# The first layer norm's sum centred before the last two parts of an output product, and the means of its weights made in small pieces

## The chip, the cores and the metric

The program runs on one core of a Trainium2 chip, in one launch. The metric is the device time of that launch in microseconds (us). The engines are named as the profile names them: PE (matrix products; PEld loads its weights), DVE, ACT and POOL (elementwise work), SP (here it only issues DMAs).

## What is computed

One step of a two-layer decoder for 576 token columns (512 of a prompt, 8 samples of 8), width 1024. Layer 0 mixes with two head groups, A (RWKV-7) and B (retention); their outputs are concatenated and go through one output product. The change sits at the end of that mixer: the output product, and the layer norm on what it adds to the residual.

```python
def layer_norm(x, g, b):
    xf = x.astype(jnp.float32)
    mu = jnp.mean(xf, -1, keepdims=True)
    var = jnp.mean(jnp.square(xf - mu), -1, keepdims=True)
    return ((xf - mu) * lax.rsqrt(var + LN_EPS)).astype(x.dtype) * g + b

y = jnp.concatenate([ya, yb], axis=-1).astype(x.dtype) @ w_out   # layer 0; ya, yb: 512 wide each
x = layer_norm(ALPHA * x + y, ln1_g[l], ln1_b[l])
x = layer_norm(ALPHA * x + sqrelu_mlp(x, w_up[l], w_down[l]), ln2_g[l], ln2_b[l])
```

## The kernel before

Activations lie with the width on the 128 partitions (8 tiles `x[0..7]`) and tokens along the free axis, in two groups of 288 columns (`g` = 0, 1). To keep float32 accuracy a factor is split into a high and a low part, and a product is three matrix products (`mm3`, lines 152 to 154: high by high, high by low, low by high). Plain float32 products (the norm's sums, the centring) go through PE in two passes.

**The mixer stage.** Twelve generators each issue one strand of work: the input projection (30 column blocks, `acc` on lines 152 to 154), the head pairs of A (`pres`, `stages`, four `back`s with the block inverse L803, the scan L863, the outputs L872/L875 and `ya`), the samples, the retention fronts and backs of B, and `wout`, the output product. `drive` steps through them. Before, the table `SCHEDULE` lists for each step which generator goes on and at which priority; the framework then orders each engine's queue by these priorities and by what is ready. An engine's queue runs strictly in order.

**The output product.** Its eight blocks k of 128 input rows come in four parts: (0, 1, 2), (3, 4, 5), (6), and 7. `Wout.part` splits the inputs of its blocks, then for each of 8 output tiles m fetches weight pieces (`wr`, two buffers; a piece is 128 x 256 or 128 x 128), splits them on ACT (L1306) and POOL (L1307), accumulates in PSUM tile `wa` and adds it to `x[m]` on DVE (L1336 in the first part, L1338 after). Part (0, 1, 2) waits for `ya2`, part (3, 4, 5) for `ya3` and the first two retention pairs, part (6) for the third. `Wout.keep`, run after the first part, fetches and splits the eight weight pieces of block 7, which stay in SBUF as `kh`, `kl`.

**The first layer norm.** `trunk` makes the products of block 7 (`acc<-hh,kh`) and hands each to `ln_add`: DVE adds it to x (L244 for m = 0, L257 for the others); for m = 0 a product over the 128 rows of `x[0]` (`cps`, L246) gives a rough mean that is taken off all eight tiles (L255: seven per group on POOL, one on DVE); then PE sums each tile (`ps`) and ACT's square of it (`pq`), both on L283. `ln_finish` makes mean and 1/deviation, then per tile subtracts and multiplies (L309 DVE, L310 POOL or DVE), scales and shifts on ACT (L313), and splits into high (L77 ACT) and low (L78 DVE).

**After it.** The first four blocks of the MLP's up product (`acc<-he,wh` and the like, 192 products of 288 columns) take x of group 0 and then of group 1; `sums` makes differences of x tiles on POOL (L1564, 16 of them), split to `ht`, `lt`; all following blocks come in pairs of seven half products (`gemm7`) that need these. The first `gemm7` product with them is `acc<-ht,wh`. `evac_up` takes relu (ACT L1588), squares (DVE L1589) and splits an up block.

Of the kernel before, what the change touches and what calls it, by code (L numbers as in the profile page):

```python
# [24 lines left out]
class Trunk:  # L25
# [252 lines left out]
    def ln_mm(self, st, n, g, t, stop):  # L278
        k = (g, n, 'ps')
        start = k not in st  # L280
        if start:
            st[k] = self.p_misc.tile([P, GN], F32, tag="misc", name='p' + n)
        self.nc.tensor.matmul(st[k], lhsT=self.ones1024, rhs=t, start=start, stop=stop)  # L283

# [938 lines left out]
def post(o):  # L1223
# [12 lines left out]
SCHEDULE = (  # L1236
# [36 lines left out]
def drive(tc, *gens):  # L1273

    base = tc.cur_priority
    for c, p in SCHEDULE:
        tc.cur_priority = base + p
        next(gens[c], None)
    tc.cur_priority = base + max(p for _, p in SCHEDULE) + 10000

# [65 lines left out]
def build(tc, i, o, coff):  # L1346
    nc = tc.nc
    T = Trunk(tc, i['w'], ahead=2)
    with ExitStack() as es:
# [9 lines left out]
        with ExitStack() as s1:  # L1359
# [121 lines left out]
            def wout():  # L1481
                for n, (ks, ns) in enumerate(WP):
# [4 lines left out]
                    if n == 0: W.keep()  # L1487
# [223 lines left out]
```

## Time and profile before

| what | us |
|---|---|
| three timed runs, median (lowest to highest) | 1575.98 (1573.06 to 1576.76) |
| the profiled execution, whole | 1570.47 |
| its span in the trace | 1568.7 |
| PE busy in the span | 1476.0 (94%) |
| DVE busy | 1077.6 (69%) |
| ACT busy | 639.8 (41%) |
| POOL busy | 564.0 (36%) |

Busy time is the union of an engine's instruction spans. Products on PE overlap each other, so the distance between the starts of two of them, and not the span of one, tells how fast they go. A number in square brackets at the end of a timeline row is the idle time of the engine before it and what ended it.

### The profile page before, as it was taken

How to read it: one execution, taken by the hardware profiler on the slowest of the kernel's cores; microseconds unless marked ns; L12 is line 12 of the kernel's file. 1: busy time of each engine (PE TensorE's matmuls, PEld its weight loads, DVE VectorE, ACT ScalarE, POOL GpSimd, SP SyncE). 2: the span in 40 equal slices, each digit the busy share in tenths (PEclk: the TensorE clock that was granted, in tenths of full speed). 3: DMA queues.
4: the chain of work that ended last, by engine and by line, in shares of the span. 5: the costliest groups of instructions: out<-in, count | busy, mean ns of one | idle time of the engine just before them, and what ended most of it. 6: DMA issues, size and time to landing. Idle time of an engine off the chain costs nothing.

```text
span 1568.7 us, 29898 instructions
## 1 busy us (share of the span) xinstructions
PE 1476.0 (94%) x11760; PEld 1421.9 (91%) x11760; DVE 1077.6 (69%) x2038; ACT 639.8 (41%) x1345; POOL 564.0 (36%) x643
## 2 busy tenths in 40 slices
PE   6999999998997889999999998989998999999995
PEld 6999898987886689999999997889988999999995
DVE  4656766675756795664846779899799575574755
ACT  4444334332233553342624545434365244251533
POOL 2032213336443551211302377555564121121355
PEclk9999999999898889999999999999999999999998
DMA  5333234435223013231322411223402314132221
GB/s 171 96 96 91 86 101 130 139 92 168 82 64 120 0 43 121 81 122 57 106 81 68 135 42 56 74 74 115 129 1 81 97 66 135 54 121 68 83 66 61
DMA packets 71197, 140.04 MB, mean 89 GB/s; under 512 B 21744, under 2 KB 31200, under 8 KB 71056
## 3 DMA queue, kind: packets, MB, share of 16 engines
q1 hardware_dynamic: 68224, 129.69, 26.6%
q0 software_dynamic: 1536, 5.57, 1.1%
q10 hardware_dynamic: 1296, 2.86, 0.6%
q8 instruction: 92, 1.51, 0.4%
q14 instruction: 49, 0.40, 0.1%
HBM read 124.39 MB, written 13.70 MB: 88 GB/s over the span
## 4 chain that ended last, share of the span: by engine, by line
PE 77%; DVE 11%; DMA 4%; POOL 4%; issue 3%; ACT 1%; SPq 1%; DVEq 0%; ACTq 0%; POOLq 0%
PE acc L152 21%; PE acc L153 21%; PE acc L154 21%; DVE wl L78 2%; PE mx L803 2%; DMA raw<-in_w 1%; DVE u L309 1%; POOL x L255 1%; DVE hl L78 1%; PE mx L700 1%; PE wa L152 1%; PE mx L542 1%; PE pq L283 1%; PE ps L283 1%; PE wa L154 1%
## 5 line engine op out<-in xcount | busy, mean ns | idle before, releaser
L77 ACT CAST wh<-raw 128x512 fp32r<-128x512 f32 x440 | 252.7, 618 | 411.2 <-PE acc L153 269.7
L78 DVE TENSOR_TENSOR wl<-raw,wh 128x512 fp32r<-128x512 f32 x440 | 330.2, 782 | 42.2 <-ACT wh L77 34.9
L153 PE MATMUL acc<-hl,wh 128*128 128x288 f32 x1180 | 349.0, 297 | 7.1 <-DVE hl L78 7.1
L154 PE MATMUL acc<-hh,wl 128*128 128x288 f32 x1180 | 348.6, 297 | 0.0
L152 PE MATMUL acc<-hh,wh 128*128 128x288 f32 x1180 | 344.4, 297 | 2.3 <-DVE ta L205 1.8
L153 PEld LDWEIGHTS acc<-hl,wh 128*128 128x128 f32 x1180 | 222.9, 189 | 8.0 <-DVE hl L78 7.5
L152 PEld LDWEIGHTS acc<-hh,wh 128*128 128x128 f32 x1180 | 221.2, 189 | 3.2 <-DVE ta L205 2.0
L154 PEld LDWEIGHTS acc<-hh,wl 128*128 128x128 f32 x1180 | 223.0, 189 | 0.3
L152 PE MATMUL acc<-xh,wh 128*128 128x288 f32 x480 | 148.3, 310 | 13.4 <-ACT xh L1395 12.4
L123 POOL TENSOR_TENSOR s<-raw 128x512 f32<-128x512 f32 x37 | 56.0, 1515 | 272.4 <-DMA raw<-in_w 206.1
L153 PE MATMUL acc<-xl,wh 128*128 128x288 f32 x480 | 146.2, 305 | 0.0
L154 PE MATMUL acc<-xh,wl 128*128 128x288 f32 x480 | 146.0, 304 | 0.0
L152 PE MATMUL acc<-ht,wh 128*128 128x288 f32 x444 | 130.9, 296 | 1.7 <-ACT wh L77 1.3
L153 PE MATMUL acc<-lt,wh 128*128 128x288 f32 x444 | 130.7, 295 | 0.0
L154 PE MATMUL acc<-ht,wl 128*128 128x288 f32 x444 | 130.5, 295 | 0.0
L123 POOL TENSOR_TENSOR raw<-raw 128x512 f32<-128x512 f32 x37 | 54.6, 1475 | 157.0 <-DVE raw L123 106.6
L152 PEld LDWEIGHTS acc<-xh,wh 128*128 128x128 f32 x480 | 91.5, 191 | 16.7 <-ACT xh L1395 12.8
L153 PE MATMUL acc<-lo,wh 128*128 128x288 f32 x352 | 105.2, 299 | 0.0
L152 PE MATMUL acc<-ho,wh 128*128 128x288 f32 x352 | 104.9, 300 | 0.1
L154 PE MATMUL acc<-ho,wl 128*128 128x288 f32 x352 | 104.9, 299 | 0.0
L153 PEld LDWEIGHTS acc<-xl,wh 128*128 128x128 f32 x480 | 91.5, 191 | 2.6 <-DVE xl L1396 0.7
L154 PEld LDWEIGHTS acc<-xh,wl 128*128 128x128 f32 x480 | 91.6, 191 | 1.5 <-issue 0.2
(461 smaller groups left out, 3498.0 us busy)
## 6 DMA issues: line engine op xcount, KB each, us to landing
raw<-in_w SPq DMA_DIRECT2D x160, 512.0 KB, 3.9
raw<-in_w SPq DMA_DIRECT2D x60, 256.0 KB, 2.9
A<-stg SPq DMA_DIRECT2D x9, 288.0 KB, 2.4
x<-in_x POOLq DMA_DIRECT2D x8, 288.0 KB, 7.4
out_y<-x SPq DMA_DIRECT2D x16, 144.0 KB, 1.8
wr<-in_w SPq DMA_DIRECT2D x16, 128.0 KB, 2.3
wr<-in_w SPq DMA_DIRECT2D x32, 64.0 KB, 2.0
kr<-A SPq DMA_DIRECT2D x6, 288.0 KB, 2.7
```

The costliest lines, as they stand in the source:

```text
L77: a = self.nc.scalar.copy(hi[:, s], src[:, s])
L78: b = self.nc.vector.tensor_tensor(out=lo[:, s], in0=src[:, s], in1=hi[:, s].bitcast(F32), op=ALU.subtract)
L123: tt = lambda e, o, x, y, op: e.tensor_tensor(out=o, in0=x, in1=y, op=op)
L152: nc.tensor.matmul(acc, lhsT=hi, rhs=xh, start=first, stop=False)
L153: nc.tensor.matmul(acc, lhsT=hi, rhs=xl, start=False, stop=False)
L154: nc.tensor.matmul(acc, lhsT=lo, rhs=xh, start=False, stop=last)
L255: e.tensor_tensor(out=t, in0=t, in1=c, op=ALU.subtract)
L283: self.nc.tensor.matmul(st[k], lhsT=self.ones1024, rhs=t, start=start, stop=stop)
L309: nc.vector.tensor_tensor(out=u, in0=r, in1=mn, op=ALU.subtract)
L542: self.nc.tensor.matmul(ps, lhsT=lhsT, rhs=rhs[:, o:o + n], start=True, stop=True)
L700: nc.tensor.matmul(both[h][:, i], lhsT=b3[q, c, h:h + 2].rearrange('p s t -> p (s t)'), rhs=la[q, c], start=True, stop=True)
L803: nc.tensor.matmul(ps[:, i], lhsT=bd(self.mb if n < 3 else self.Y0, j + i), rhs=v[:, j + i], start=True, stop=True)
```

## The change

1. **Order.** `SCHEDULE` is gone; `drive` now keeps a clock for each generator, adds `RATE[c]` times what a step yields, and always steps the generator with the lowest clock that isn't waiting. For the generators other than `wout` the yields are unchanged, the resulting order is not that of the table.
2. **Means of weights.** `keep` becomes `means`, which yields between its pieces: eight pieces of two 128 x 128 blocks for the row sums of blocks 6 and 7 over all 1024 outputs (DVE reduce), then four more for block 7, from which ACT takes the mean (bias) before they are split and kept. Part (6) fetches four such double pieces and takes the mean off on ACT, where it fetched eight single ones.
3. **Centring.** After part (3, 4, 5), `center` sums each group's eight x tiles on PE against a matrix of 1/1024 and DVE takes that mean off all 16. As the weights of what is added later have no mean, x stays centred.
4. **First norm.** `ln0_add` adds, squares on ACT, adds squares in pairs on POOL for m < 6, and sums on PE five tiles per group; no `cps`, no `ps`. `ln0_finish` scales x in one DVE operation a tile, and takes high (ACT), low (DVE) and the shifted x (ACT) from it.
5. `evac_up` squares on ACT.

```diff
-SCHEDULE = (
-    (0, 100000), (1, 100000), (1, 100000), (2, 100000), (3, 100000), (4, 100000), (5, 100000), (6, 100000), (7, 100000), (8, 100000), (9, 100000), (10, 100000), (11, 100000),
...
+RATE = (735.4, 69, 94, 102.8, 96.9, 129.4, 147, 133, 167.5, 137.3, 134, 148.1)
...
+    while live:
+        ok = [c for c in live if free(c)]
+        c = min(ok, key=lambda c: (max(time[c], now) if wait[c] is not None else time[c], c))
...
+        else: time[c] += RATE[c] * (1 if y is None else y)
...
+    def ln0_add(self, st, m, g, r, a):
+        nc = self.nc
+        st[g, m] = r
+        nc.vector.tensor_tensor(out=r, in0=r, in1=a, op=ALU.add)
+        t = self.p_tmp.tile([P, GN], F32, tag="t", name="lt", bufs=self.tb)
+        nc.scalar.activation(t, r, AF.Square)
+        if m >= 6: self.ln_mm(st, 'q', g, t, m == 7)
+        elif m % 2:
+            nc.gpsimd.tensor_tensor(out=t, in0=st[g, 'q'], in1=t, op=ALU.add)
+            self.ln_mm(st, 'q', g, t, False)
+        else: st[g, 'q'] = t
+
+    def ln0_finish(self, st, g, par, out):
...
+        with self.tc.issue_after(self.pre.ins):
+            nc.scalar.activation(w0, v, AF.Ln, bias=self.eps)
+        nc.scalar.activation(w, w0, AF.Exp, scale=-0.5)
+        V.scalar_tensor_tensor(out=w0, in0=w, scalar=-0.5, in1=w, op0=ALU.mult, op1=ALU.mult)
+        V.scalar_tensor_tensor(out=v, in0=v, scalar=LN_EPS, in1=w0, op0=ALU.add, op1=ALU.mult)
+        V.scalar_tensor_tensor(out=v, in0=v, scalar=1.5, in1=w, op0=ALU.add, op1=ALU.mult)
+        gam, bet = par
+        for m in range(KT):
+            r, (hi, lo), b = st[g, m], out(m, g), bet[:, m:m + 1]
+            V.scalar_tensor_tensor(out=r, in0=r, scalar=gam[:, m:m + 1], in1=v, op0=ALU.mult, op1=ALU.mult)
+            x = nc.scalar.activation(hi, r, AF.Identity, bias=b)
+            y = V.scalar_tensor_tensor(out=lo, in0=r, scalar=b, in1=hi.bitcast(F32), op0=ALU.add, op1=ALU.subtract)
+            nc.scalar.activation(r, r, AF.Identity, bias=b)
+            if g and m == self.gated - 2: self.gate = [x.ins, y.ins]
...
-    def keep(self):
-        self.w7 = [self.weights(m, 7, 1, True) for m in range(8)]
+    def means(self):
...
+        for k in (6, 7):
+            s = self.wq.tile([P, 4], F32, name=f's{k}', bufs=1)
+            for m in range(0, 8, 2):
+                t = load(k, m)
+                yield 3
+                nc.vector.tensor_reduce(out=s[:, m // 2:m // 2 + 1], in_=t, axis=AX.XY, op=ALU.add)
+            b = self.wq.tile([P, 1], F32, name=f'b{k}', bufs=1)
+            nc.vector.tensor_reduce(out=b, in_=s, axis=AX.X, op=ALU.add)
+            nc.vector.tensor_scalar(out=b, in0=b, scalar1=-1.0 / 1024, scalar2=None, op0=ALU.mult)
+            self.less[k] = b
+        for m in range(0, 8, 2):
+            t = load(7, m)
+            yield 3
+            hi, lo = (self.wq.tile([P, 2, P], F32R, name=f'k{c}{m}', bufs=1) for c in 'hl')
+            nc.scalar.activation(t, t, AF.Identity, bias=b)
+            nc.scalar.copy(hi, t)
+            nc.gpsimd.tensor_tensor(out=lo, in0=t, in1=hi.bitcast(F32), op=ALU.subtract)
+            self.w7 += [(hi[:, x], lo[:, x]) for x in range(2)]
+
+    def center(self, mx):
...
+        for g in range(2):
+            ps = mx.tile([P, 512], F32, tag='mx', name='mx')[:, 0:GN]
+            xs = [t[:, GN * g:GN * (g + 1)] for t in T.x]
+            for m, t in enumerate(xs):
+                nc.tensor.matmul(ps, lhsT=o, rhs=t, start=m == 0, stop=m == KT - 1)
+                if m % 2: yield 1
+            for t in xs: nc.vector.tensor_tensor(out=t, in0=t, in1=ps, op=ALU.subtract)
+            yield 3
...
-                    if n == 0: W.keep()
+                    if n == 0: yield from W.means()
+                    if n == 1: yield from W.center(mxb)
...
-        nc.vector.tensor_tensor(out=t, in0=t, in1=t, op=ALU.mult)
+        nc.scalar.activation(t, t, AF.Square)
```

What moves on the engines shows best at three places. First PE, where part (3, 4, 5) of the output product begins. Before (`L542` is the gate product of pair 3's `ya`, `hd` with L969 the normed output of a retention pair; `L1074` transposes the next retention pair):

```order
L154 MATMUL wa<-hi_4610,l 128x288
L542 MATMUL mx<-gd,lw 128x288
L1131 MATMUL rpo<-rS,e 128x128
L542 MATMUL mx<-gd,lw 128x288
L969 MATMUL mx<-cst_170,hd 128x128 x4
L971 MATMUL mx<-cst_170,hd 128x64
L1160 MATMUL mx<-rvt,rkm 64x64 x16
L944 MATMUL mx<-cst_170,rot 64x128
L152 MATMUL wa<-hi_5490,h 128x288 x2
L1074 MATMUL mx<-cst_170,w_5345 128x128 x4
L153 MATMUL wa<-lo_5491,h 128x288 x2
```

Now, at the same place (L904 and L907 are the pair's outputs `po`, before L872 and L875; L1001 and L1003 a retention pair's; L524 transposes pair 3's normed output, L574 is its gate product):

```order
L154 MATMUL wa<-hi_5010,l 128x288
L904 MATMUL po<-uv_127,lr_126 64x64 x16
L907 MATMUL po<-la_125 64x64 x14
L1001 MATMUL mx<-cst_170,hd 128x128 x4
L1003 MATMUL mx<-cst_170,hd 128x64
L524 MATMUL mx<-cst_170,hd 64x64 x18
L574 MATMUL mx<-gd,lw 128x288 x2
L152 MATMUL wa<-hi_5693,h 128x288 x2
L153 MATMUL wa<-lo_5694,h 128x288
L154 MATMUL wa<-hi_5693,l 128x288
L152 MATMUL wa<-hi_5697,h 128x288
```

All other rows of the mixer now stand ahead of part (3, 4, 5); before, the last retention pair's stood between its products. Between pair 3's `po` and the part's first product PE now has 25 products.

Second PE, at the end of part (6). Before:

```order
L152 MATMUL wa<-hi_5921,h 128x288
L153 MATMUL wa<-lo_5922,h 128x288
L154 MATMUL wa<-hi_5921,l 128x288
L246 MATMUL cps<-x_4548,o_6126 128x288
L283 MATMUL ps<-x_4548,o_6125 128x288
L283 MATMUL pq<-lt,o_6125 128x288
L283 MATMUL ps<-x_4549,o_6125 128x288
L152 MATMUL acc<-hh_6160,kh_5486 128x288
```

Now:

```order
L152 MATMUL wa<-hi_6013,h 128x288
L153 MATMUL wa<-lo_6014,h 128x288
L154 MATMUL wa<-hi_6013,l 128x288
L283 MATMUL pq<-lt,o_6153 128x288 x10
L152 MATMUL acc<-he_6160,wh 128x288 x4
L153 MATMUL acc<-le_6161,wh 128x288
L154 MATMUL acc<-he_6160,wl 128x288
L152 MATMUL acc<-ho_6168,wh 128x288
```

The products of block 7 now stand among those of part (6), ahead of this place, and ten sums of squares are all that stands between the last `wa` and the up product.

Third DVE, from the last addition to x of each version on. Before:

```order
L1338 TENSOR_TENSOR x_4555<-x_4555,wa 128x288 x2
L255 TENSOR_TENSOR x_4548<-x_4548,ln 128x288
L257 TENSOR_TENSOR x_4549<-x_4549,acc 128x288
L257 TENSOR_TENSOR x_4550<-x_4550,acc 128x288
L257 TENSOR_TENSOR x_4551<-x_4551,acc 128x288
L257 TENSOR_TENSOR x_4552<-x_4552,acc 128x288
```

Now:

```order
L289 TENSOR_TENSOR x_4262<-x_4262,acc 128x288
L305 SCALAR_TENSOR_TENSOR w_6303<-w 128x288
L306 SCALAR_TENSOR_TENSOR pq<-pq,w_6303 128x288
L307 SCALAR_TENSOR_TENSOR pq<-pq,w 128x288
L311 SCALAR_TENSOR_TENSOR x_4255<-x_4255,par,pq 128x288
L311 SCALAR_TENSOR_TENSOR x_4256<-x_4256,par,pq 128x288
L311 SCALAR_TENSOR_TENSOR x_4257<-x_4257,par,pq 128x288
```

The additions of block 7 (L289) are done by then for both groups, and group 0's eight scalings (L311) and eight low parts (L313) follow without a subtraction; then come the three operations L305 to L307 and the same sixteen of group 1.

More of the change, by code (lines that the diff above doesn't have):

```diff
@@ L283, in ln_mm @@
         self.nc.tensor.matmul(st[k], lhsT=self.ones1024, rhs=t, start=start, stop=stop)
+    def ln0_add(self, st, m, g, r, a):
[10 more added lines that the diff above has]
+    def ln0_finish(self, st, g, par, out):
+        nc, V = self.nc, self.nc.vector
+        pt, v = self.p_tmp, st[g, 'q', 'ps']
+        w0, w = [pt.tile([P, GN], F32, tag="t", name=n, bufs=self.tb) for n in ('w0', 'w')]
+        with self.tc.issue_after(self.pre.ins):
[12 more added lines that the diff above has]
+            if g and m == self.gated - 2: self.gate = [x.ins, y.ins]
     def ln_finish(self, st, g, par, out, last=False):
@@ L1233, in post, with free @@
             c(sh[1:][None]), c(wk(o['swkv'])), c(rt(o['sret'])), c(cv[1:][None]))
-SCHEDULE = (
[33 rows of a table removed]
-)
-def drive(tc, *gens):
[L1275 to L1279, printed above, removed]
+RATE = (735.4, 69, 94, 102.8, 96.9, 129.4, 147, 133, 167.5, 137.3, 134, 148.1)
+def drive(tc, *gens):
+    base, n = tc.cur_priority, len(gens)
+    time, wait, live, held, now = [100000.0] * n, [None] * n, set(range(n)), set(), 100000.0
+    def free(c):
+        w = wait[c]
+        return w is None or (w() if callable(w) else w not in held)
+    while live:
+        ok = [c for c in live if free(c)]
+        c = min(ok, key=lambda c: (max(time[c], now) if wait[c] is not None else time[c], c))
+        if wait[c] is not None:
+            time[c] = max(time[c], now)
+            if not callable(wait[c]): held.add(wait[c])
+            wait[c] = None
+        now = max(now, time[c])
+        tc.cur_priority = base + int(time[c])
+        try:
+            y = next(gens[c])
+        except StopIteration:
+            live.discard(c)
+            continue
+        if callable(y): wait[c] = y
+        elif isinstance(y, tuple):
+            if y[0] > 0: wait[c] = y[1]
+            else: held.discard(y[1])
+        else: time[c] += RATE[c] * (1 if y is None else y)
+    tc.cur_priority = base + int(max(time)) + 10000
 CFG = {(n, g): dict(ds=() if n else tuple(range(8)), dq=() if n else tuple(range(8)), sv=(7,), qv=(7,), pg=(1, 2, 3, 4, 5, 6, 7), mulv=(0, 3, 6), affv=()) for n in range(4) for g in range(2)}
@@ L1298, in __init__, with weights @@
         self.T, self.nc, self.w = T, T.nc, w
-        self.w7 = []
+        self.w7, self.less = [], {}
         self.y = [None] * 8
-    def weights(self, m, k0, n, keep=False):
-        t = self.wq.tile([P, 2 * P], F32, tag='wr', name='wr', bufs=2)[:, 0:n * P]
-        self.nc.sync.dma_start(t, self.w[30 + m, :, P * k0:P * (k0 + n)])
-        hi, lo = (self.wq.tile([P, n * P], F32R, name=f'k{c}{m}', bufs=1) if keep else self.wq.tile([P, 2 * P], F32R, tag=f'w{c}', name=c, bufs=2)[:, 0:n * P] for c in 'hl')
+    def weights(self, m, k0, n):
+        t = self.wq.tile([P, 2, P], F32, tag='wr', name='wr', bufs=2)
+        b = self.less.get(k0)
+        if b is None:
+            t = t[:, 0:n]
+            self.nc.sync.dma_start(t.rearrange('p m c -> p (m c)'), self.w[30 + m, :, P * k0:P * (k0 + n)])
+        else:
+            n = 2
+            self.nc.sync.dma_start(t, self.w[30 + m:32 + m, :, P * k0:P * (k0 + 1)].rearrange('m p c -> p m c'))
+            self.nc.scalar.activation(t, t, AF.Identity, bias=b)
+        hi, lo = (self.wq.tile([P, 2, P], F32R, tag=f'w{c}', name=c, bufs=2)[:, 0:n] for c in 'hl')
         self.nc.scalar.copy(hi, t)
@@ L1308, in weights, with load @@
         return hi, lo
-    def keep(self):
-        self.w7 = [self.weights(m, 7, 1, True) for m in range(8)]
+    def means(self):
+        nc = self.nc
+        def load(k, m):
+            t = self.wq.tile([P, 2, P], F32, tag='wr', name='wr', bufs=2)
+            nc.sync.dma_start(t, self.w[30 + m:32 + m, :, P * k:P * (k + 1)].rearrange('m p c -> p m c'))
+            return t
+        for k in (6, 7):
[17 more added lines that the diff above has]
+    def center(self, mx):
+        nc, T = self.nc, self.T
+        o = self.wq.tile([P, P], F32, name='wo', bufs=1)
+        nc.gpsimd.memset(o, 1 / 1024)
+        for g in range(2):
[6 more added lines that the diff above has]
+            yield 3
     def part(self, ks, first):
@@ L1328, in part @@
                 n = min(2, len(ks) - j)
-                hi, lo = self.weights(m, ks[j], n)
+                if ks[j] not in self.less: hi, lo = self.weights(m, ks[j], n)
+                elif m % 2 == 0: two = self.weights(m, ks[j], n)
+                if ks[j] in self.less: hi, lo = (w[:, m % 2:m % 2 + 1] for w in two)
                 for g, a in enumerate(accs):
                     for x in range(n):
-                        T.mm3(a, hi[:, P * x:P * (x + 1)], lo[:, P * x:P * (x + 1)], *[c[:, GN * g:GN * (g + 1)] for c in h[ks[j + x]]], j + x == 0, j + x == len(ks) - 1)
+                        T.mm3(a, hi[:, x], lo[:, x], *[c[:, GN * g:GN * (g + 1)] for c in h[ks[j + x]]], j + x == 0, j + x == len(ks) - 1)
             for g, a in enumerate(accs):
@@ L1510, in build @@
             T.ones1024 = hp.tile([P, P], F32, name='o1'); T.ones128 = hp.tile([P, P], F32, name='o2')
+            T.eps = hp.tile([P, 1], F32, name='ep'); nc.gpsimd.memset(T.eps, LN_EPS)
             nc.gpsimd.memset(T.ones1024, 1 / 1024); nc.gpsimd.memset(T.ones128, 1 / 128)
@@ L1611, in mlp @@
             T.gemm(u + 16 * q + 8, 8, hx, res_evac(T.ln_state(ln, x), lnpar(ln), out, first=q == 0, final=q == 3), tail=TL if q == 3 else 0, far=(FAR1 if ln == 1 else 0) if q == 3 else 0)
-    ev = res_evac(T.ln_state(0, x), lnpar(0), split_x, first=False)
+    st = T.ln_state(0, x)
     T.ensure(E0)
@@ L1618, in trunk @@
             T.mm3(a, hi, lo, *hx(7, g), True, True)
-            ev(m, g, a)
+            T.ln0_add(st, m, g, x[m][:, gs[g]], a)
+        T.ln0_finish(st, g, lnpar(0), split_x)
     T.ensure(41)
```

32 rows, old and new, of the table SCHEDULE are left out of this document.

## The prediction

> **What bounds the kernel now.** First the page: PE is busy nearly throughout, so time can only come out of the places where it isn't, or out of its own work.
>
> ```profile
> span 1568.7 us, 29898 instructions
> PE 1476.0 (94%) x11760; PEld 1421.9 (91%) x11760; DVE 1077.6 (69%) x2038; ACT 639.8 (41%) x1345; POOL 564.0 (36%) x643
> ```
>
> Then the table of busy time by stretch, from the end of the input projection to where PE is full again. Columns: stretch, its length, busy us of PE, PEld, DVE, ACT, POOL (instructions), granted clock of PE.
>
> ```profile
> 314.00:353.50 39.50, 36.78 (x398) 33.06 (x398) 27.65 (x73) 12.79 (x34) 14.49 (x23) 0.91 0.34 93
> 353.50:366.10 12.60, 8.43 (x97) 7.91 (x96) 3.23 (x8) 3.69 (x9) 8.13 (x12) 1.00 0.93 325
> 366.10:443.00 76.90, 69.25 (x761) 61.95 (x761) 52.11 (x133) 25.40 (x72) 39.22 (x54) 0.88 0.28 81
> 443.00:470.00 27.00, 26.42 (x219) 24.49 (x219) 14.61 (x42) 7.73 (x25) 10.75 (x18) 0.89 0.24 70
> 470.00:497.00 27.00, 20.41 (x144) 16.87 (x143) 21.59 (x52) 10.91 (x26) 8.11 (x15) 0.93 0.46 139
> 497.00:523.00 26.00, 19.77 (x74) 13.86 (x75) 15.37 (x31) 8.20 (x19) 15.77 (x18) 0.83 0.10 36
> 523.00:543.00 20.00, 20.00 (x118) 18.31 (x116) 11.73 (x24) 10.44 (x26) 5.01 (x6) 0.89 0.00 1
> 543.00:562.80 19.80, 12.28 (x79) 11.67 (x77) 19.80 (x20) 13.03 (x31) 19.80 (x20) 0.88 0.00 1
> ```
>
> Two parts show. Up to 497 PE works off the mixer's end and the output product, with small holes. From 497 to 563 it is busy for 52 of 66 us, and in the last stretch DVE and POOL are busy without a pause: there the norm, not PE, sets the pace. The timelines of DVE and PE bound that stage:
>
> ```profile
> 496.49 0.93 DVE L1338 TENSOR_TENSOR x<-x,wa 128x288 f32<-128x288 f32 x2
> 511.36 0.46 DVE L294 SCALAR_TENSOR_TENSOR ln<-pq,d 128x288 f32<-128x288 f32 x1 [4.36 <-ACT d L292]
> 523.12 1.57 PE L152 MATMUL acc<-he,wh 128*128 128x288 f32 x4
> 562.79 0.61 PE L153 MATMUL acc<-hl,wh 128*128 128x288 f32 x1 [4.72 <-DVE hl L78]
> 571.48 0.41 PE L152 MATMUL acc<-ht,wh 128*128 128x288 f32 x1
> ```
>
> The last addition of part (6) ends at 497.42. Group 0's sums take until 511.4, the first up product starts at 523.1, and the 192 products of the four unpaired blocks are done only when the first `ht` product starts, at 571.48. So the stage takes **74.1 us**. What PE must do in it shows in the distance of starts:
>
> ```profile
> 541.13 0.29 PE L153 MATMUL acc<-lo,wh 128*128 128x288 f32 x1
> 541.26 0.29 PE L154 MATMUL acc<-ho,wl 128*128 128x288 f32 x1
> 507.02 0.65 PE L283 MATMUL ps<-x,o 128*128 128x288 f32 x2
> 507.51 0.65 PE L283 MATMUL pq<-lt,o 128*128 128x288 f32 x2
> ```
>
> A product of 288 columns takes 0.133 us, a plain float32 one (two passes) 0.49.
>
> **The norm's stage, worked anew.** It removes both `cps` and their chain, 16 `ps`, six of 16 `pq`, the subtractions L255 and L309 and the products L310; on PE 24 products of 0.49 us, 11.8 us. What is left, from the last addition on, is priced by these rows:
>
> ```profile
> 499.76 0.44 ACT L260 ACTIVATE lt<-x 128x288 f32<-128x288 f32 x1 [0.53 <-DVE x L255]
> 537.51 0.45 ACT L299 ACTIVATE w<-w 128x288 f32<-128x288 f32 x1
> 511.73 1.92 DVE L309 TENSOR_TENSOR u<-x,ln 128x288 f32<-128x288 f32 x5
> 517.08 1.04 DVE L309 TENSOR_TENSOR u<-x,ln 128x288 f32<-128x288 f32 x1
> 518.05 0.44 DVE L257 TENSOR_TENSOR x<-x,acc 128x288 f32<-128x288 f32 x1
> ```
>
> Square 0.44, sum on PE 0.65 (the row of `pq`), logarithm and exponential 0.45 each, three DVE operations of 0.46 (the row of L294), eight scalings (five take 1.92, so 3.0), the first low part 0.46: 6.9 us, with hand-overs between engines some 7.5. Then 192 products of 0.133, 25.5 us: **33 us** if nothing holds PE. What does is the way to `ht`. POOL's 16 differences need x of both groups, shifted by ACT:
>
> ```profile
> L1564 POOL TENSOR_TENSOR ts<-x,ts 128x288 f32<-128x288 f32 x8 | 8.9, 1132 | 0.0
> L1564 POOL TENSOR_TENSOR ts<-x 128x288 f32<-128x288 f32 x4 | 4.3, 1075 | 0.0
> L1564 POOL TENSOR_TENSOR ts<-x,x 128x288 f32<-128x288 f32 x4 | 4.0, 1010 | 0.0
> L123 POOL TENSOR_TENSOR raw<-raw 128x512 f32<-128x512 f32 x1 | 1.5, 1476 | 0.0
> L78 DVE TENSOR_TENSOR lt<-ts,ht 128x576 fp32r<-128x576 f32 x8 | 5.6, 746 | 0.0
> ```
>
> ACT's queue holds 37 operations or so between the first exponential (at 2.9 us) and the first shifted tile of group 1 (eight squares, sixteen high parts, eight shifts, the other group's two, some relus): at 0.4 us, 18 us. Then POOL 17.2 and one L123, 1.5, then the last `lt` 0.7: 37.4; I take **38 us**, a saving of **36**. The low end of the stage is PE's 33. For the high end: while POOL runs, a DVE operation on two SBUF tiles takes 1.04 where 0.37 is its pace alone (L309 above), one that reads PSUM stays at 0.44 (L257 between). DVE's queue has about 66 operations from the last addition to the last `lt`; half of them slowed gives 33 x 0.37 + 33 x 1.04 = 47, so 50 with the start. The saving lies between 24 and 41.
>
> The squares of `evac_up` leave DVE for ACT, which is busy 13 of 19.8 us where DVE has no pause; that is in the 38. At the second MLP I cost the same eight at nothing: only PE's queue of ready products covers them there, and without it they are worth eight times the 0.45 row, under 4 us.
>
> **The mixer's end.** Three terms move the last addition.
>
> Centring: 16 plain products of 0.49 on PE, **+7.8 us**, as PE is the busy engine there (26.4 of 27 us in 443 to 470). The 16 subtractions on DVE (0.44 each) run beside part (6)'s first products and those of block 7; uncovered, the eight of group 1 would cost 3.5.
>
> A hole before part (3, 4, 5): now nothing but 25 small products stands on PE between pair 3's `po` and the part's first product. How long the way takes shows on the timelines of PE and DVE before, where it was filled:
>
> ```profile
> 419.06 1.03 PE L875 MATMUL po<-la 64*64 64x64 f32 x28
> 420.14 0.69 DVE L989 TENSOR_REDUCE hs<-po 128x8 f32<-128x512 f32 x1 [0.38 <-PE po L875]
> 440.98 1.15 PE L1160 MATMUL mx<-rvt,rkm 64*64 64x64 f32 x32 [2.69 <-ACT hd L972]
> 443.08 0.85 PE L152 MATMUL wa<-hi,h 128*128 128x288 f32 x2 [0.62 <-ACT h L1306]
> ```
>
> From 420.1 to 443.1, 23 us of reductions, `rsqrt`, transposes, gate and splits. Now DVE has less else to do there and the 25 products fill some 2: I take **+15 us**; ends 0 (other work slips in) and 23. What stood in this place before has moved ahead and is done there, so only the idle time counts.
>
> Holes that close: before part (0, 1, 2) PE sat for its first input, and in the row above for `hd`:
>
> ```profile
> 366.10 0.54 PE L152 MATMUL wa<-hi,h 128*128 128x288 f32 x2 [4.17 <-ACT hi L1322]
> ```
>
> Both waits now have mixer rows ahead of them: 4.2 + 2.7, **-6.9 us**, or nothing.
>
> The pieces of the means: `keep` and the last pieces of the first part ran as one string of DMA issues, part (3, 4, 5) as another.
>
> ```profile
> 423.94 17.18 SPq L1304 DMA_DIRECT2D wr<-in_w x12
> 445.81 12.09 SPq L1304 DMA_DIRECT2D wr<-in_w x8
> ```
>
> 1.43 and 1.51 us each. Twelve pieces of `means` instead of eight add 4 x 1.5 = 6 us to that string, part (6) gives four back; a double piece with runs of 512 B isn't in the trace, between the 1.4 above and twice that. I cost it at nothing, since `means` stands beside pair 3's scan and the wait just priced; uncovered it is 6 to 20 us. Behind these issues in SP's queue stand the pieces of part (3, 4, 5) and the trunk's `raw` loads. The eight reductions, at most 0.69 us of DVE each by the 128 x 512 row of their kind (L989), hide there too.
>
> PE's clock after a hole bears on this: in 497 to 523 the granted clock is 0.83, and the four products from 523.12 take 1.57 us, not 0.69 as at full pace (three distances of 0.133 and the last one's 0.29). The Trainium skill ("TensorE: Matmul & The Clock Gate", "Part 1: The HAM clock gate (the "warmup" mystery)") says the clock halves after some 3.4 us idle and needs about 3.4 us of work to come back; that speaks against a change that leaves PE idle in two places. By it each costs 1.7 us, as an estimate, and the sum would be 3.4 us less of a gain; the trace agrees with the slow start.
>
> **The sum.** 7.8 + 15 - 6.9 = +15.9 at the mixer's end, -36 in the norm's stage: **-20.1 us**. The profiled execution took 1570.47 (span 1568.7 and 1.8 around it), so 1550.4; the three runs' median, 1575.98, is 5.5 above it, and against that **1556**. With the ends of its terms this case reaches from 1541 to 1573.
>
> **Rivals.**
>
> *The hole is covered*: other strands, or the means' work, fill PE while `ya` of pair 3 is made. For it: before, that stretch was 90% busy. Against: the queue is in order and holds nothing else. 7.8 - 6.9 - 36 = -35: 1541. Chance 0.22.
>
> *The gain is eaten*: DVE beside POOL sets the stage (24 saved), the hole is whole. 7.8 + 23 - 6.9 - 24 = 0: 1576, no change. The 1.04 us rows speak for it, DVE's shorter list against. Chance 0.12.
>
> *Slower, by the new order*: the table goes, and pair 2's scan now stands behind the last projection product instead of ahead of it. Before:
>
> ```profile
> 311.82 0.33 PE L863 MATMUL ch<-la 64*64 64x64 f32 x4
> 330.17 0.48 PE L863 MATMUL ch<-la 64*64 64x64 f32 x4
> L153 PE MATMUL acc<-xl,wh x480: 289/294/608, 7.6 to 353.4; 128*128 128x288 f32 x160
> ```
>
> The scan took 19 us under the projection's products, which ran until 353.4. Without them PE may sit through those 19 us; with the whole hole (23) and no hole closed: 7.8 + 23 + 19 - 36 = +14, **1590**. It decides once the mixer's end slips by more than the 36 saved. For it: retention and samples are all that is left to fill. Against: pair 3's inverse now runs beside that scan. Chance 0.14. That the sums are not saved at all is ruled out by PE's order.
>
> Forecast 0.52. A measurement of this kernel can tell about 0.3%, 4.7 us. Faster by more: 0.52 + 0.22 = 0.74; within: 0.12; slower: 0.14. The range takes in the better case with some us below it and stops halfway up the slower one: 1534 to 1583.
>
> **What the profile will show.** Right if from the last addition to x (L289) to the first `ht` product it is 33 to 45 us; if PE idles 10 us or more ahead of part (3, 4, 5); if that last addition lies 10 to 22 us later than 497. Wrong if PE's idle time between 300 and 450 grows by more than the hole (the order costs more than the norm gives), if weight pieces end the waits of part (3, 4, 5) (the means aren't covered), or if `lt` ends PE's longest wait with the stage near 50 us.

## The result, and the profile after

The changed kernel takes **1596.13 us** (median of 4 runs, 1591.37 to 1608.08), the kernel before 1574.95 us beside it (4 runs, 1573.06 to 1576.76): a ratio of 1.0144, with a 95% interval of 1.0097 to 1.0192. It is slower by 21 us (15 to 30 by the interval; its runs took 1591.4, 1591.8, 1600.5 and 1608.1 us), where 20 less were forecast. The profiled execution took 1591.37 us; the head of its page:

```profile
span 1589.6 us, 29855 instructions
PE 1486.1 (93%) x11744; PEld 1430.3 (90%) x11744; DVE 1064.8 (67%) x2040; ACT 645.8 (41%) x1355; POOL 547.8 (34%) x619
```

PE has 16 records of products fewer than before (eight plain float32 products, each in two passes), and is busy 10 us longer; the span grew by 20.9. To find where, the same two points as in the prediction, on the timelines of DVE and PE after (start, us, engine, line, operation):

```profile
547.63 0.45 DVE L1406 TENSOR_TENSOR x<-x,wa 128x288 f32<-128x288 f32 x1
548.11 0.45 DVE L289 TENSOR_TENSOR x<-x,acc 128x288 f32<-128x288 f32 x1
586.53 0.29 PE L152 MATMUL acc<-ht,wh 128*128 128x288 f32 x1
```

The last addition to x ends at 548.6 instead of 497.4: **51 us later**, where 16 were forecast. From there to the first `ht` product it takes **38.0 us** instead of 74.1, the number that was forecast. That makes 15.0 of the 20.9; the other 5.9 come behind the first `ht` product. Groups of PE's products with their waits, two before and one after, each over the 54 us from the first `ht` product on (busy us, mean ns of one | idle us ahead of them, and its end):

```profile
L152 PE MATMUL acc<-ht,wh 128*128 128x288 f32 x24 | 7.3, 304 | 1.4 <-ACT wh L77 1.3
L153 PE MATMUL acc<-lt,wh 128*128 128x288 f32 x24 | 7.1, 295 | 0.0
```
```profile
L153 PE MATMUL acc<-lt,wh 128*128 128x288 f32 x24 | 7.5, 312 | 4.0 <-DVE lt L78 4.0
```

So PE reaches the `ht` products earlier than POOL and DVE can feed the rest of them. In the first 13.5 us it waits 2.6 us longer than before, its clock is 0.87 instead of 1.00, and it makes 61 products instead of 90: some 4 us of the saving go there. Where the other 2 go was not followed.

What sets the 38.0 us is PE itself. Its first up product starts 9.0 us after the last addition (557.5), and from there to the first `ht` product it makes 216 products without a pause, 29.0 us. POOL's last difference ends at 591.2 and the last `lt` at 597.1, 48.6 us after the last addition.

Where the 51 us lie is told by the stretch from 250 us to the projection's last product, and from that to the first product of part (3, 4, 5). Before, then after (columns as in the prediction's table; behind the clock stand the DMA share and GB/s):

```profile
250.00:353.50 103.50, 100.78 (x1133) 93.19 (x1132) 78.75 (x185) 34.27 (x83) 39.20 (x48) 0.97 0.41 118
353.50:443.00 89.50, 77.68 (x858) 69.86 (x856) 55.34 (x141) 29.09 (x80) 47.35 (x66) 0.90 0.37 115
```
```profile
250.00:349.50 99.50, 93.79 (x816) 85.34 (x815) 62.74 (x144) 35.09 (x80) 35.67 (x45) 0.97 0.38 111
349.50:489.90 140.40, 111.80 (x1234) 97.25 (x1232) 85.00 (x240) 39.75 (x107) 52.67 (x72) 0.78 0.32 96
```

The second stretch grew by **50.9 us**, which equals the slip (the first is 4.0 us shorter, and from part (3, 4, 5)'s first product to the last addition it takes 58.7 us instead of 54.4, with the centring in it). It holds 376 products more than before. By their lines 208 of them belong to one head pair (its scan, outputs, norm, gate and samples), and 20 to a retention pair; these had run between the products of the projection (that stretch has 317 fewer; the others ran earlier, before 250 us) and now run after them, when there is nothing else to put between them. 147 are the last retention pair's, which before stood behind the start of part (3, 4, 5). Of the 50.9 us, 16.8 are PE's idle time (28.6 instead of 11.8) and 34.1 are busy time, at a granted clock of 0.78 instead of 0.90. The scan of pair 2 shows it on PE's timeline: before, its first and last row stood at 311.8 and 330.2, under the projection; after:

```profile
373.67 0.48 PE L895 MATMUL ch<-la 64*64 64x64 f32 x4
393.98 0.31 PE L895 MATMUL ch<-la 64*64 64x64 f32 x3
```

Behind it come pair 3's scan (its last `ch` at 456.3) and its output, and then the hole that was forecast:

```profile
469.78 1.76 PE L907 MATMUL po<-la 64*64 64x64 f32 x28
476.49 1.09 PE L1001 MATMUL mx<-cst,hd 128*128 128x128 f32 x4 [4.95 <-DVE hd L997]
481.61 2.19 PE L524 MATMUL mx<-cst,hd 64*64 64x64 f32 x36 [3.73 <-DVE hd L1038]
486.36 2.29 PE L574 MATMUL mx<-gd,lw 128*128 128x288 f32 x4 [2.57 <-ACT hd L1047]
489.91 0.85 PE L152 MATMUL wa<-hi,h 128*128 128x288 f32 x2 [1.25 <-ACT hi L1388]
```

From `po`'s end (471.5) to the part's first product it is 18.4 us, with 12.5 us of waits in brackets: a chain of DVE and ACT operations with small products between, and no other work on PE to fill the waits.

### The profile page after: what moved, and what is told of

Same layout as the page of the kernel before. It is cut to its first block, busy times and chain, and to the rows that moved or that the text cites. A ratio compares the mean times of both kernels' runs of the same rounds, so it can differ in the third digit from the quotient of the medians.

```text
span 1589.6 us, 29855 instructions
## 1 busy us (share of the span) xinstructions
PE 1486.1 (93%) x11744; PEld 1430.3 (90%) x11744; DVE 1064.8 (67%) x2040; ACT 645.8 (41%) x1355; POOL 547.8 (34%) x619
## 4 chain that ended last, share of the span: by engine, by line
PE 71%; DVE 12%; DMA 6%; POOL 4%; issue 3%; ACT 3%; SPq 1%; ACTq 0%; DVEq 0%; POOLq 0%
PE acc L152 19%; PE acc L153 19%; PE acc L154 19%; DVE wl L78 3%; DMA wr<-in_w 2%; PE mx L835 2%; DMA raw<-in_w 2%; DVE u L341 1%; PE mx L732 1%; PE wa L152 1%; POOL s L123 1%; PE wa L153 1%; PE wa L154 1%; ACT wh L77 1%; SPq L814 1%
```

## Experiments

Two theories stood against each other. **A**: the order costs it, as the table is replaced by rates and the pairs' chains are issued later. **B**: the new work costs it, the centring, the pieces of means and the hole that they make. All times below are medians beside runs of the kernel before on the same chip (1572.5 to 1573.8 us in the sets).

**The order alone.** The kernel before, with nothing but this (`drive` as in the change):

```diff
-SCHEDULE = (
...
-)
+RATE = (735.4, 69, 94, 102.8, 96.9, 129.4, 147, 133, 167.5, 137.3, 134, 148.1)
 def drive(tc, *gens):
...
```

> The kernel before with the planner's rates in place of the written table, nothing else changed: the same products, the same norm. Theory A (the order costs it): the mixer's end slipped by 51 us with the whole change, of which the centring's 16 products explain 8 and the hole ahead of part (3, 4, 5) some 15; the other 28 are the order's, and the hole is the order's too, so the last addition of part (6) comes 28 to 43 us later than 497 and the time is 1603 to 1618 us. Theory B (the new work costs it: centring, pieces of means and the hole they make; the order is nothing): 1570 to 1580 us, the last addition within 5 us of 497.

1606.5 us, ratio 1.0214 (1.0193 to 1.0235): **+33.5 us**. Its last addition ends at 533.2, its norm's stage is 73.8 us long, as before. The same stretches, of this run:

```profile
250.00:351.30 101.30, 97.21 (x828) 88.47 (x827) 62.98 (x145) 35.03 (x80) 37.01 (x45) 0.95 0.39 110
351.30:485.20 133.90, 110.56 (x1232) 96.42 (x1231) 83.30 (x228) 38.52 (x107) 53.70 (x75) 0.79 0.30 93
```

The 1232 products behind the projection are there without a centring or a mean. From part (3, 4, 5)'s first product to the last addition this run takes 48.0 us instead of 54.4, as the last retention pair is out of that stretch; the 33.5 us are the balance. Theory A stands; B falls for the larger part.

**The whole change with the old table**, 22 steps of `wout` (strand 11) added to its 424: twelve (11, 125228) for the means, ten from 129375 on for the centring.

```diff
-RATE = (735.4, 69, 94, 102.8, 96.9, 129.4, 147, 133, 167.5, 137.3, 134, 148.1)
+SCHEDULE = (
...
+)
```

> The whole change, but the strands are driven by the old table: its 424 steps with their times, 12 steps for the pieces of means put at one time behind the first part of the output product, 10 for the centring behind the second part at the planner's distances, the third part that much later. Theory A: the norm's stage still gives 32 (36 less the 4 us that PE then waits for lt), the centring costs 8, the hole 0 to 15: 1551 to 1566 us, the last addition 8 to 23 us later than 497. Theory B: as the changed kernel, 1585 to 1600 us, the last addition near 548.

1564.8 us, ratio 0.9949 (0.9931 to 0.9966). It was run again as the base of a later set:

> The run with the old table kept, unchanged, once more beside the three others of this set: 1561 to 1567 us by every theory; it is the base to which they are compared.

1562.1 us, ratio 0.9926 (0.9909 to 0.9943). So the change gains 8 to 11 us once the order is kept, and this version is faster than both kernels. In the first of these runs the last addition ends at 517.3 and the first `ht` product starts at 555.5, in the second at 521.3 and 559.4; part (3, 4, 5) starts at 453.6 and 457.7. It is the same kernel, so a point on a single trace is good to some 4 us; the stretch between these two points agrees (63.7 and 63.6 us). With the pieces of means spread in the table:

> As the run with the old table kept, but the 12 pieces of means stand 148 ns of plan apart instead of at one time, and the two later parts of the output product 1776 ns of plan later. Theory A: 1551 to 1566 us, within 5 us of the run with the pieces at one time, since the pieces wait for nothing on PE. Theory B: 1585 to 1600 us. If the pieces of means do hold up part (3, 4, 5) by their loads, the two runs differ by more than 5 us.

1563.1 us, ratio 0.9945 (0.9927 to 0.9962): no difference.

**Which of the strands.** In the plan of the old table the second halves of pairs 2 and 3 (strands 5 and 6) end at 118642 and 123833, by the rates at 126152 and 131794. Two numbers were halved, first in the run with the order alone, then in the changed kernel:

```diff
-RATE = (735.4, 69, 94, 102.8, 96.9, 129.4, 147, 133, 167.5, 137.3, 134, 148.1)
+RATE = (735.4, 69, 94, 102.8, 96.9, 64.7, 73.5, 133, 167.5, 137.3, 134, 148.1)
```

> The run with the order alone (before, driven by rates: 1606.5 us), with the rates of two strands halved, those of the second halves of pairs 2 and 3 (129.4 to 64.7, 147 to 73.5). In the old table these two end at 118642 and 123833, under the rates at 126152 and 131794. Theory A1 (the order costs because these two chains are planned late, so that they run behind the projection's last product instead of under it): most of the 33 us comes back, 1573 to 1585 us, and the stretch from the projection's end to the first product of part (3, 4, 5) falls from 136 to under 105 us. Theory A2 (the cost is spread over the order of all strands, or it is the late start of the first part of the output product): 1595 us or more.

> The changed kernel (1596.1 us) with the same two rates halved, its output unchanged. Theory A1: most of the 33 us of the order comes back, 1563 to 1576 us. Theory A2: 1585 us or more.

1581.3 us, ratio 1.0053 (1.0032 to 1.0073), and 1570.8 us, ratio 0.9978 (0.9964 to 0.9993). Beside the kernel before that is +8.3 instead of +33.5 and -2.2 instead of +21.2: **25 and 23 us less**, as A1 expected. The stretches of the first:

```profile
250.00:358.50 108.50, 102.74 (x1033) 93.19 (x1033) 72.29 (x175) 38.14 (x88) 37.70 (x48) 0.95 0.36 108
358.50:453.10 94.60, 77.52 (x811) 69.04 (x810) 58.78 (x142) 29.91 (x81) 51.86 (x70) 0.86 0.37 115
```

The way from the projection's end to part (3, 4, 5) is 95 us with 811 products, near the 89.5 us and 858 products of the kernel before, and the projection ends 7 us later than with the order alone for what it now covers. Which strands make the last 8 us wasn't tried.

**The norm's stage alone.** The kernel before with its table, and of the change only `ln0_add`, `ln0_finish`, their calls and the squares on ACT; it leaves out the subtraction of all means of the first norm.

> The kernel before, table and all, with the norm's new stage alone (no sums of x, squares of the relu on ACT); the means of the weights and of the sum are not subtracted, so the first norm's output is not centred. Theory A: the stage is worth 32 to 36 us by itself, 1539 to 1546 us, with the last addition at 497 as before and the first ht product near 535. Theory B says nothing else of this run. A third theory, that the stage was short in the changed kernel only because ACT, DVE and the loads had more time ahead of it (the mixer's end came 51 us later), expects a stage of 50 us or more here and 1555 us or more.

1547.7 us, ratio 0.9845 (0.9828 to 0.9862): **-25.3 us**, not 32 to 36. The stage is 40.4 us, so it saves 33.7, and the third theory falls; but the last addition ends later than before. Its timelines (PE, PE, DVE, PE):

```profile
445.05 0.53 PE L152 MATMUL wa<-hi,h 128*128 128x288 f32 x2 [0.80 <-ACT h L1338]
489.65 1.06 PE L152 MATMUL acc<-hh,kh 128*128 128x288 f32 x6
505.10 0.81 DVE L289 TENSOR_TENSOR x<-x,acc 128x288 f32<-128x288 f32 x2
546.29 0.29 PE L152 MATMUL acc<-ht,wh 128*128 128x288 f32 x1
```

Part (3, 4, 5) starts 2.0 us later than before, which is no more than two executions of one kernel differ by; the last addition ends 8.5 us later, at 505.9. The stretch from the one to the other, before and in this run:

```profile
443.00:497.40 54.40, 46.84 (x360) 41.36 (x360) 36.61 (x93) 18.64 (x51) 18.86 (x33) 0.91 0.35 106
```
```profile
445.05:505.90 60.85, 53.41 (x389) 47.58 (x390) 42.65 (x107) 21.45 (x58) 22.80 (x38) 0.87 0.33 108
```

It grew by 6.5 us, all of it busy time on PE: 29 products more, and a clock of 0.87 instead of 0.91. The products are those of block 7 (`acc<-hh,kh`). Before, nine of their 16 groups of three ran from 502.9 us on, among the norm's sums and thus inside the 74.1 us; now all stand ahead of the point from which the stage is counted (27 x 0.133 = 3.6 us at full pace). A wait of 3.6 us for `lt` behind the first `ht` products takes the next part. (The two profiled executions differ by 20.2 us, the medians by 25.3.)

**The squares back on DVE**, in the kernel with the old table.

> The run with the old table kept, with the squares of the relus of the unpaired blocks back on DVE (L1659 as before the change), all else the same. Theory F1 (DVE beside POOL sets the norm's stage, so its eight operations more cost there): 2 to 5 us more than the base, the stage from the last addition to the first ht product 40 to 43 us instead of 38. Theory F2 (POOL's 16 differences, fed by ACT, set it; the squares on ACT cost or give nothing): within 2 us of the base, the stage within 1 us of 38.

1566.7 us, ratio 0.9959 (0.9945 to 0.9973), 4.6 us above the base of its set, with intervals that just don't overlap (0.9909 to 0.9943 there); above the first run of the base it is 1.9. The stage grew by 0.7 us only, to 38.8; so F1 has the size and not the place. At and behind its first `ht` product PE waits four times, 0.5, 1.1, 1.4 and 1.9 us, where the base waits once, 3.9. From the last addition to the end this trace is 4.0 us longer than the base's: 0.7 in the stage, some 2.3 (17 products fewer) in the 80 us behind it, the rest later.

**The centring.** In the kernel with the old table it was left out, made twice (its start and stop flags and its steps fitted to the sixteen), and made without its subtraction (the first and last leave the sum uncentred):

```diff
-                    if n == 1: yield from W.center(mxb)
```
```diff
-            for m, t in enumerate(xs):
+            for m, t in enumerate(xs + xs):
```
```diff
-            for t in xs: nc.vector.tensor_tensor(out=t, in0=t, in1=ps, op=ALU.subtract)
+            nc.vector.tensor_copy(out=o2[:, g:g + 1], in_=ps[:, 0:1])
```

> The run with the old table kept (1564.8 us), but the sum for the first norm is not centred: no 16 products, no 16 subtractions; the means of the weights stay. Theory C1 (each added product costs its own time, as PE is the busy engine): 7.8 us less, 1555 to 1559 us. Theory C2 (the 16 products fill gaps between the last parts; in the traces the way from part (3, 4, 5) to the last addition grew by 3 us only): 1560 to 1564 us.

> The run with the old table kept, with the 16 products of the centring issued twice (the second eight of each group write the same sums anew), to be set beside the same kernel with them once and the run without them. Theory C1 (each product costs its own 0.49 us): 7.8 us more than with them once. Theory C2 (they fill gaps): 4 us more at most.

> The run with the old table kept, the 16 products of the centring made but their sum not subtracted: one column of it is copied instead, 16 operations of 0.37 us on DVE fewer. Theory H1 (part (6) waits for the string, 3.7 us): that wait goes and the time is 3 to 4 us less than the base (1562 to 1565 us in three sets), 1558 to 1561 us; most of the centring's 5 us is then the string's, not the products'. Theory H2 (the wait has another end, or comes back later): 1562 us or more.

Left out: 1557.9 us, ratio 0.9911 (0.9893 to 0.9929). Twice: 1567.2, ratio 0.9966 (0.9954 to 0.9978). Without its subtraction: 1560.1, ratio 0.9905 (0.9886 to 0.9924). The centring thus costs 4 to 7 us by the two bases, the same 16 products a second time 2 to 5, and without the subtraction it costs nothing that can be told from leaving it out. Left out alone, the time falls where C1 expected it; the doubled run (C2) and the run without the subtraction (H1) speak against C1. So the first 16 products seem to find room in PE's gaps, and the price is mostly DVE's string; the sizes are no better than the 3 us of the intervals, and beside the second base only the doubled run stands clear. The string shows in the second run of the base, on DVE's and on PE's timeline:

```profile
498.25 5.91 DVE L1392 TENSOR_TENSOR x<-x,mx 128x288 f32<-128x288 f32 x16
504.08 0.44 DVE L1422 TENSOR_TENSOR x<-x,wa 128x288 f32<-128x288 f32 x1
```
```profile
504.26 0.58 PE L152 MATMUL acc<-hh,kh 128*128 128x288 f32 x1 [3.75 <-issue]
```

PE's next product there is the first of block 7, and it starts 0.1 us after the last subtraction's end (504.16), when part (6)'s first addition has only begun. In the changed kernel the same wait is 3.75 us too, and there the profile names the subtraction (`[3.75 <-DVE x L1376]`). So PE waits for the string itself. The likely tie is read from the code and was not tested: the accumulators `acc` take over the PSUM of the mixer's tiles, and the sum lies in one of these. Without the subtractions PE's longest wait between 480 and 515 us is 1.3. The wait has a tail: behind it the products stand 0.24 us apart instead of 0.133 until about 510.

**The pieces of means.** In the kernel with the old table: neither made nor subtracted; made but not subtracted; zeros subtracted without making them (all three leave the means of these weights in).

> The run with the old table kept (1564.8 us), but the means of the weights are neither made nor subtracted: the eight weight pieces of block 7 are loaded singly as before, block 6 singly too; the centring stays. Theory D1 (the pieces of means stand ahead of part (3, 4, 5) in the queue of weight pieces and hold it up: its first product came 8.6 us later than without them): 1554 to 1559 us, the first product of part (3, 4, 5) near 445. Theory D2 (the pieces are covered): 1562 to 1567 us, that first product within 2 us of 453.6.

> The run with the old table kept (1562.1 and 1564.8 us in two sets), with the means of the weights made as there (eight more loads, sums on DVE) but not subtracted from the weight pieces of blocks 6 and 7 (eight operations fewer on ACT). Theory G1 (the pieces cost by being made): no change, 1561 to 1565 us. Theory G2 (they cost by the subtraction, another step between a weight piece's landing and its high part): 1554 to 1558 us.

> The run with the old table kept, with zeros subtracted from the weight pieces instead of their means, which are not made: eight loads and ten small DVE operations fewer. Theory G1: 1554 to 1558 us, the first product of part (3, 4, 5) 5 us or more earlier than 457. Theory G2: 1561 to 1565 us.

1555.5 us, ratio 0.9895 (0.9880 to 0.9910); 1559.0, ratio 0.9909 (0.9895 to 0.9924); 1553.9, ratio 0.9883 (0.9869 to 0.9898). So they cost about **8 us** (7 to 9 by the two bases). Not making them saves 8 to 11 us, as G1 expected; not subtracting them saves 3 to 6, between G1 and G2 and not clear of the second base. The three don't add up, and they differ by more than the means: ahead of part (3, 4, 5) and in part (6) the base fetches 12 and 4 double pieces, the first of these runs 8 and 8 single ones, the zeros' run 4 and 4 double ones. On PE's timelines the first product of part (3, 4, 5) shows what is made, in the base (second run) and in the zeros' run:

```profile
457.68 0.61 PE L152 MATMUL wa<-hi,h 128*128 128x288 f32 x1 [0.59 <-ACT h L1349]
```
```profile
441.05 0.85 PE L152 MATMUL wa<-hi,h 128*128 128x288 f32 x2 [2.22 <-ACT hi L1398]
```

In the other two it starts at 451.5 (neither made nor subtracted) and 455.8. The way to it shows on SP's queue, where the part's first weight pieces (L1343) go out; the base, then the zeros' run:

```profile
450.04 1.03 SPq L1360 DMA_DIRECT2D wr<-in_w  x2
455.00 4.26 SPq L1343 DMA_DIRECT2D wr<-in_w  x4
```
```profile
427.18 5.58 SPq L1360 DMA_DIRECT2D wr<-in_w  x4
436.27 5.32 SPq L1343 DMA_DIRECT2D wr<-in_w  x3
```

In the base the last two pieces of means (L1360) hold both buffers `wr` until POOL has their low parts (`kl`); SP waits 3.9 us for that, and the part's first product follows 2.7 us behind its first weight piece.

**Their place.** The same pieces between the steps of part (0, 1, 2) (`means` then goes on behind each piece):

```diff
-                    yield from W.part(ks, n == 0)
-                    if n == 0: yield from W.means()
+                    for j, y in enumerate(W.part(ks, n == 0)):
+                        if j > 2:
+                            for _ in range(2 - j % 2): next(ms, None)
+                        yield y
```

> The run with the old table kept (1564.8 us), with the 12 pieces of means made between the eight steps of part (0, 1, 2), one or two behind each, instead of all behind its last; the same work and output. Theory D1 (the pieces cost by their place: twelve loads and their conversions in the queue right ahead of part (3, 4, 5), 9 us when they were left out): most of the 9 us comes back, 1554 to 1559 us, and the first product of part (3, 4, 5) moves from 453.6 to near 445. Rival D3 (they cost by what they are: the two buffers for weight pieces, ACT's and POOL's conversions, wherever they stand): 1562 us or more, as part (0, 1, 2) is now held up by them.

1561.1 us, ratio 0.9926 (0.9909 to 0.9943), 1 us less than the base of its set: D1 falls as far as the time goes. Part (3, 4, 5) does start near 445, as D1 had it, 7 to 11 us earlier than in the base, but part (6) then waits longer:

```profile
446.56 0.50 PE L152 MATMUL wa<-hi,h 128*128 128x288 f32 x2
494.16 0.61 PE L152 MATMUL wa<-hi,h 128*128 128x288 f32 x1 [6.45 <-DVE x L1422]
```

From the first of these rows to the last addition it takes 72.0 us instead of 63.6. 52 products more lie in that stretch, which in the base stand ahead of the part; of the 8.4 us 3.2 are busy time and 5.2 idle.

To see whether that wait alone took the gain, the subtractions were to be spread over part (6)'s steps, in the base and in this run:

```diff
-            for t in xs: nc.vector.tensor_tensor(out=t, in0=t, in1=ps, op=ALU.subtract)
+            self.ps.append(ps)
...
+                if self.ps: nc.vector.tensor_tensor(out=r, in0=r, in1=self.ps[g], op=ALU.subtract)
```

> The run with the old table kept, with the 16 subtractions of the centring made one by one ahead of part (6)'s additions to the same block instead of in one string ahead of them all; the same work and output. Theory H1 (part (6) waits 3.7 us for an accumulator because its first addition stands behind the whole string of 5.9 us on DVE): that wait goes, 1558 to 1561 us. Theory H2 (DVE's work is the same and only moves the wait to the last additions): 1561 to 1565 us.

> The run with the pieces of means between the steps of part (0, 1, 2) (1561.1 us), with the subtractions step by step as well. Theory H1 (what the earlier place gave was lost in the wait of 6.45 us behind the string of subtractions): 1553 to 1557 us, and no wait over 2 us ahead of part (6). Theory H2: 1559 us or more.

1564.0 us, ratio 0.9951 (0.9938 to 0.9964), and 1560.8, ratio 0.9934 (0.9918 to 0.9950). Both are inconclusive, as the edit didn't do what it was for. DVE's timeline in the first:

```profile
501.13 5.91 DVE L1419 TENSOR_TENSOR x<-x,mx 128x288 f32<-128x288 f32 x16
506.97 0.44 DVE L1423 TENSOR_TENSOR x<-x,wa 128x288 f32<-128x288 f32 x1
```

Written one by one ahead of each addition, the 16 still stand in one string; all are ready as soon as their sum is, so the framework most likely issued them as they became ready. The run without subtractions, above, was made for that reason.

## Why the prediction was wrong

By its own terms, against the runs that hold one of them each:

| term | predicted | measured |
|---|---|---|
| order: hole before part (3, 4, 5) and holes that close | +15 - 6.9 = +8.1 | +33.5 (order alone) |
| the norm's stage | -36 | -25.3 (alone) |
| centring | +7.8 | +4 to 7 (left out) |
| pieces of means | 0 | +8 (left out) |
| sum | -20.1 | some +22; the change itself +21.2 (15 to 30) |

- **The order is the step that failed.** It was costed by holes alone: "What stood in this place before has moved ahead and is done there, so only the idle time counts." The runs showed the reverse: behind the projection's end stand 376 products more, 228 of which had run under it, and of the 50.9 us that this stretch grew by 34.1 are busy time and 16.8 idle. The order alone costs 33.5 us. The hole itself was sized well (18.4 us with 12.5 of waits, against 15, with ends 0 and 23), and the two holes that were to close did, though others opened (4.4 us at 359.3, 5.1 at 467.9). What was missing in the sum is the work that had been under the projection and now had nothing beside it.
- **The slower rival had the cause and nearly the point.** It said that pair 2's scan would stand behind the last projection product, at +14 and 1590 us, and decide "once the mixer's end slips by more than the 36 saved". The end slipped by 51. It priced the scan as 19 us of idle PE; most of what was measured is busy time instead. The argument against it, that pair 3's inverse runs beside that scan, was true (its products stand between the scan's from 375 to 392) and worth little: both are chains of small products. It got 0.14; halving two rates shows that the order of these two pairs makes 25 of the 33 us.
- **The norm's stage** is 38.0 us as forecast, and that is luck. The forecast got there by ACT, POOL and the last `lt` (37.4 us); that path took 48.6. PE, put at 33 us, set it: 9.0 instead of 7.5 us to the first up product, and 216 products instead of 192 before the first `ht` one (216 before the change too, a miscount of 3.2 us). As a term the stage was too large by some 11: 27 products of block 7 were inside the 74.1 us before and are outside the 38, and no term of the sum paid for them (6.5 us, with the clock that they met); 3.6 to 4.0 us come back as a wait for `lt` behind the first `ht` product. With DVE and POOL as the bound, a shorter way to the first `ht` is not a shorter way to the last.
- **The centring** was of the right size for another reason than given: not 16 products on PE, which find gaps, but the string of subtractions on DVE, which was costed at nothing as it would run "beside part (6)'s first products"; uncovered it was put at 3.5, and the wait is 3.75 us, with slow products behind it.
- **The pieces of means** were put at nothing, with 6 to 20 us if uncovered; they cost 8. That they stand by "pair 3's scan and the wait just priced" didn't cover them: with the old table their last pieces hold the buffers that part (3, 4, 5)'s weights wait for. The earlier place starts that part 7 to 11 us earlier and loses 8.4 behind it, to products that it has overtaken and to idle time, the longer wait of part (6) above all. That this wait could be had back was not shown.
- The upper end of the forecast case, 1573, doesn't follow from its terms (24 saved gives 1568 with the hole at 15 and 1576 with it at 23); nothing rests on it.
- Of the signs that were named, the stage (38.0) and the hole (over 10 us) came out as forecast, and the last addition did not. The sign against, that PE's idle time between 300 and 450 us would grow by more than the hole, was badly chosen: in that window PE was busy 134.9 us before and 136.5 after. Moved work shows as more products, not as idle time.

## What to carry to other kernels

When a hand-made order is dropped along with an edit, run the order alone first: count the instructions of each engine on both sides of the last long piece of work that can cover them, not only the idle time. Here a chain of small products, each waiting for the one before, cost little under the projection's stream and some 25 us behind it, by two rates; so such chains are to be planned early. When a stage is measured from an event, see which work crosses that event in the new order, or it is paid by no term.

## What the runs showed of the hardware that was not expected

PE's granted clock fell to half without a pause. In the kernel before, PE's waits between 380 and 409 us are at most 0.5 us, and yet:

```profile
392.00:394.00 2.00, 1.34 (x38) 1.24 (x38) 1.90 (x12) 0.21 (x1) 0.14 (x1) 1.00 0.45 100
396.00:398.00 2.00, 2.00 (x20) 1.72 (x21) 0.00 (x0) 0.00 (x0) 1.33 (x2) 0.50 0.00 0
402.00:404.00 2.00, 2.00 (x14) 1.54 (x14) 0.42 (x1) 0.51 (x2) 0.97 (x3) 0.50 0.63 102
```

It stays there from about 395 to 404.6 us, some 9 us of products with hardly a pause, about half of that time the dense ones of part (0, 1, 2), after a stretch of small ones (outputs of 64 x 8 to 64 x 64). The Trainium skill ("TensorE: Matmul & The Clock Gate", "Part 1: The HAM clock gate (the "warmup" mystery)") has the clock fall after an idle window of about 3.4 us and come back after about 3.4 us of sustained work; this trace shows it fall without such a window and come back later. Behind the hole of the changed kernel the half clock lasts from the part's first product at 489.9 to about 495.8, with products on PE without a break but for one pause of 0.63 us:

```profile
492.00:494.00 2.00, 2.00 (x10) 2.00 (x10) 0.76 (x1) 0.09 (x2) 0.00 (x0) 0.50 0.79 207
494.00:496.00 2.00, 2.00 (x10) 1.76 (x10) 0.80 (x2) 1.35 (x3) 0.73 (x1) 0.56 1.02 418
496.00:498.00 2.00, 2.00 (x15) 1.75 (x14) 2.00 (x5) 1.90 (x5) 0.84 (x1) 1.00 0.61 231
```

At half pace these 5.9 us are some 2.6 lost, as an estimate, where the prediction gave 1.7 by that page. What sets the clock between such stretches was not tried.
